# GpSimd's subtraction for the lower parts of the weights: four instructions of 256 columns instead of one of 1024

## The chip, the cores and the metric

The kernel runs on one core of a Trainium2 chip. The metric is device time in microseconds. The kernel before has a median of 3354.24 us over 3 runs (3351.83 to 3357.93).

## The reference

A sequence of 512 tokens with 1024 features passes two blocks of two layers each, all in float32. A layer of block 1 has RMS norms, one wide input product, rotary positions, windowed attention with sinks, compressed, selected and windowed attention with gates, two branch products mixed by gates, an output product with a norm behind it, and a feed-forward with a causal convolution of width 3 over 5632 channels, GELU and gate. A layer of block 2 has a state-space part (a convolution of width 7, a chunked scan in both directions, gate and norm), windowed attention with a relative bias, an output product over both, and a gated feed-forward. What matters here:

```python
def hybrid_layer(x, ...):                       # block 1, called for each of 2 layers
    h = rms_norm(x, attn_pre_gain)
    u = h @ w_in
    ...
    x = x + rms_norm(mixed @ w_out, attn_post_gain)
    h = rms_norm(x, ffn_pre_gain)
    x = x + rms_norm(conv_ffn(h, ffn_w_up, ffn_conv_w, ffn_conv_b, ffn_w_down), ffn_post_gain)
```

## The kernel before

The activations are kept transposed, as tiles of 128 features by 512 tokens. A product of float32 precision is made of three products of a reduced type: each operand is an upper part (`h`, `wh`) and a lower part (`hl`, `wl`), and `mm3` (lines 488 to 490) adds upper by upper, lower weight by upper, upper weight by lower into one bank of PSUM.

The weights come as 460 chunks of 128 x 1024, eight tiles of 128 x 128 each, in the order in which TensorE takes them. The class `Stream` handles them. `load` (line 301) issues a chunk's DMA on the SyncE queue into one of four raw buffers; `conv` makes the upper part by a copy on ScalarE (line 314), or on GpSimd while `busy["act"]` is set, in some stretches with attention (line 312), and then the lower part, raw minus upper, on GpSimd (line 315). Both parts have four buffers. `next` is called for each tile; at the first tile of chunk c it loads up to chunk c + 6 and converts up to chunk c + 3, and it hands slices of 128 columns of both parts to `mm3`.

The order of instructions on every engine is the order in which the program writes them; the waits between engines are put in by the framework. GpSimd's queue holds, beside the chunks, a share of the element-wise work: one tap of the width-7 convolution (line 1410), the scan's decays `adm`, weights `xw` and sums `xd` (lines 1628, 1544, 1643, 1684), rotary products (828), lower parts of some activations (400), and every second residual add behind a norm (1341).

The places that the prediction speaks of: `Squares.add` (line 421, closing add 424) sums the squares of the feature tiles on VectorE; `sums` (433) adds them over the features on TensorE (`stat`); `rstd_a` (442 to 455) takes one over the root by eleven small VectorE instructions of four columns behind a reduction; `spread` (472) broadcasts it to all partitions on TensorE (`statb`). In `dense_group` the squares come while the first products of four output tiles run, and the broadcast comes five weight tiles into the next product. In the convolution of block 2 the taps are the VectorE instructions of line 1416, ScalarE applies the activation (1421) and TensorE transposes the result (`xtp`, 1520). In the scan TensorE makes `gp` (1658), for which a bank has to be free that VectorE reads (`xd`, 1695). In block 1 `sk` (1102), `KL` (639) and `gx` (1181) are VectorE instructions of the attention and of the mixing, and `sp` and `mh` are a product and an operand that come behind such instructions.

Of the kernel before, what the change touches and what calls it, by code (L numbers as in the profile page):

```python
# [10 lines left out]
F32 = mybir.dt.float32  # L11
# [6 lines left out]
T = 512  # L18
# [5 lines left out]
NSLOT = 66              # working tiles of 128 x T  # L24
NB, NO = 2, 2           # output tiles taken together where the last factor comes late
XD = 30                 # tiles of weights before the first heads' queries are split
GA, GB, GC = 1, 4, 1    # tiles of weights before, between and within the gated products
NWU, NKW = 13, 6        # products that keep the clock up: at the start, at a norm
# [6 lines left out]
# ------------------------------------------------------------------ weight stream  # L35
# [8 lines left out]
def _plan():  # L44
    """128x128 weight tiles in the order in which the tensor engine takes them."""
# [103 lines left out]
# ------------------------------------------------------------------ constants of the shapes  # L149
# [37 lines left out]
def _onehot():  # L187
    """Bucket of each relative position -255..255 (t5, bidirectional); row 32 marks the outside."""
    oh = np.zeros((33, 512), np.float32)
    for i in range(512):  # L190
        rel = i - 255
        if i == 511 or abs(rel) > 128:
            oh[32, i] = 1
            continue
        n = abs(rel)
        b = n if n < 8 else 8 + sum(n * n >= 64 * 2 ** k for k in range(1, 8))
        oh[(16 if rel > 0 else 0) + min(b, 15), i] = 1
    return oh
# [48 lines left out]
def trunk_kernel(ctx: ExitStack, tc: tile.TileContext, xT, positions, wts, cst_d, oh_d, rb_d, cw1_d,  # L247
# [20 lines left out]
    # the eight banks of PSUM in turn; a bank that is held stays out until it is free again  # L268
# [16 lines left out]
    # ---------------------------------------------------------------- weights  # L285
    class Stream:
# [18 lines left out]
        def conv(self, upto):  # L305
            while self.conved < min(upto, NCHUNK):
                c = self.conved
                r = self.raw.pop(c)
                h = wpool.tile([128, CH * 128], F32R, tag="wh", name="wh", bufs=4)
                lo = wpool.tile([128, CH * 128], F32R, tag="wl", name="wl", bufs=4)  # L310
                if busy["act"]:
                    G.tensor_copy(h, r)  # L312
                else:
                    A.activation(h, r, AF.Copy)  # L314
                G.tensor_sub(lo, r, h.bitcast(F32))  # L315
                self.hl[c] = (h, lo)
                self.conved += 1

        def defer(self, n, fn):
            """fn after n more tiles of weights."""  # L320
            self.later.append((self.t + n, fn))
# [26 lines left out]
        def drip(self, gen):  # L348
            """One step of gen for each tile of weights from now on."""
            def f():  # L350
                if next(gen, self) is not self:
                    self.defer(1, f)
            self.defer(1, f)
# [3 lines left out]
    # ---------------------------------------------------------------- constants  # L357
# [38 lines left out]
    def split(h, lo, src, eng_l=None, scale=None):  # L396
        """h + lo == src (times the column scale), each in 12 significant bits."""
        if scale is None:
            A.activation(h, src, AF.Copy)  # L399
            (eng_l or V).tensor_sub(lo, src, h.bitcast(F32))  # L400
        else:
            A.activation(h, src, AF.Identity, bias=0.0, scale=scale)  # L402
            V.scalar_tensor_tensor(lo, src, scale, h.bitcast(F32), op0=OP.mult, op1=OP.subtract)  # L403

    class Squares:
        """Squares summed over the feature tiles; the last tile stays one of its own where it comes late."""
# [19 lines left out]
        def sums(self, upto):  # L426
            """The sums over the features of a tile, [token of a block, block], for the tiles that are there."""
# [9 lines left out]
    def rstd_a(sq, n, act=False):  # L437
        """1/sqrt(mean + eps) of each token, [token of a block, block]."""
# [19 lines left out]
    def warm_sqrt():  # L458
        """Brings the table of the square root in ahead of its use."""
        A.activation(small(1, "warm"), epst, AF.Sqrt)  # L460

    def keep_warm(n):
        """Products that keep the tensor engine's clock up while it waits."""
# [4 lines left out]
    def spread(r4):  # L468
        """[token of a block, block] to [any partition, token], in PSUM."""
# [22 lines left out]
    def dense(keys, hs, evac):  # L492
        """One output tile; yields after each tile of the contraction."""
# [12 lines left out]
    def dense_parts(keys, hs, cut, evacs):  # L506
        """Some output tiles: the first part of the contraction for each of them, then the rest."""
# [11 lines left out]
    def dense_group(keys, hs, evacs, sq, store, x=None, after=None):  # L519
        """Four output tiles, the contraction outermost: it starts with the first tile of hs.  The factor of the  # L520
        norm (of the squares sq, of x where they are still to come) and what follows from it come a little into
        the next product."""
# [30 lines left out]
    def prep(x, gcol, late=False):  # L553
        """Gain and split of a tile, and its square for the norm; as a function of the tile's number."""
# [32 lines left out]
    def run_units(units, lags, fill, per, tail=0, prep=()):  # L587
        """Stage k of unit u comes at step u + lags[k]; the filler goes in between (per: steps per unit, tail:
        steps of the filler for each step after the last unit; prep: pieces of work, each with its first step)."""
# [25 lines left out]
    def pieces_of(gen, n):  # L615
        """A generator's n pieces as functions."""
        return [lambda: next(gen, None)] * n

    def stack_q(X, h, get):
        """One of a pair of heads as a tile of its two parts: products over all 128 rows; in two pieces."""  # L620
# [7 lines left out]
    def stack_k(K, g, get):  # L628
        """Keys of one of a pair of groups: their upper part and their lower part, each twice; in four pieces."""
# [19 lines left out]
    def head_units(h, score, ranges, order, vt, o, final):  # L649
        """The four units of a head: the scores of each block of queries; then for each block of keys (ranges: the  # L650
        queries that see it) the probabilities transposed, in two parts, and their product with the two parts of
        the values, side by side, over all those queries at once.  order: the keys, such that each of these
        products either adds to sums of all its queries or, the bank's marks cleared by the first one, starts them
        all.  o["t"][its half] becomes the
        product, [features, tokens]."""
# [57 lines left out]
    def widen(o, den):  # L713
        """A factor of each token, [token of a block, block and head], for each feature."""
# [3 lines left out]
    def spread_pair(o):  # L718
        """A pair of heads, [features, tokens], times their factors."""
# [11 lines left out]
    def value_parts(pt, s, name):  # L731
        """Values of one of a pair of groups, [tokens of a block, block, upper and lower part]."""
# [10 lines left out]
    # ================================================================ block 1  # L743
# [39 lines left out]
    def layer1(l, x, hs, sq, gnext, side):  # L783
# [48 lines left out]
        def tokens(src, name):  # L832
            """[features, tokens] to [tokens of a block, block, features]."""
# [5 lines left out]
        # ---- compressed keys and values  # L839
        cmp = {}  # L840

        def windows(src):
            """The tokens 16 n + 2 i + (0 or 1) of each group of heads, with the position added."""
# [70 lines left out]
        def cmp_scores(i):  # L914
            """Softmax over the compressed blocks, times the gate, transposed; all heads of a block."""
# [42 lines left out]
        def head(src, h):  # L958
            """The two pieces that make head h's tile; the source goes after the second head of the pair."""
# [7 lines left out]
        # ---- projections  # L967
# [63 lines left out]
        # ---- fillers  # L1031
# [20 lines left out]
        # ---- attention units  # L1052
# [10 lines left out]
        def halves(name):  # L1063
            """Half a tile; the other half goes to the next call."""
# [6 lines left out]
        def score_of(h, X, K, mask, k0, init, nm, den, last):  # L1071
            """Exponentials of the scores of a block of queries, not yet normed, and their first block of keys."""
# [16 lines left out]
        # sliding window with sinks  # L1089
# [42 lines left out]
        # selected blocks (all of them are selected) and window, both causal  # L1132
# [41 lines left out]
        # ---- branches, output, post norm  # L1174
# [40 lines left out]
        # ---- feed forward  # L1215
# [85 lines left out]
    def later(i, gated):  # L1301
        """The gated products of the pairs that are there, in steps a little into the products that follow."""
# [4 lines left out]
    class Acts:  # L1307
        """Eleven of the gated products, each taken when it is there."""
# [20 lines left out]
    def post_norm(x, ys, gcol, sq, gnext, side):  # L1329
        """x += norm(ys); its split for the products that follow, and the squares of the norm before them."""  # L1330
# [17 lines left out]
    # ================================================================ block 2  # L1348
    bias_d = dpool.tile([128, 16, 384], F32, name="bias_d")

    def bias_table():
        """Bias by relative position, laid out as [query of a block, head, key of three blocks]."""
# [34 lines left out]
    def layer2(l, x, hs, sq, gnext):  # L1387
# [58 lines left out]
        # ---- dt and decays, [token of a chunk, chunk, direction and head]  # L1446
# [64 lines left out]
        # ---- x to tokens  # L1511
# [46 lines left out]
        # ---- chunked scan, both directions  # L1558
# [38 lines left out]
        def advance(prev, c, g, d, xw):  # L1597
            """State after the chunk from the state before it (None: zero)."""
# [172 lines left out]
        # ---- windowed attention; the state space half of the output product fills in  # L1771
# [69 lines left out]
        # ---- feed forward  # L1841
# [101 lines left out]
    # ================================================================ program  # L1943
# [67 lines left out]
```

## Time and profile before

| | |
|---|---|
| median of 3 runs | 3354.24 us |
| profiled execution, span (its own time) | 3354.5 us |
| TensorE busy (PE) | 3132.5 us, 93%, 14604 products |
| VectorE busy (DVE) | 2145.5 us, 64% |
| ScalarE busy (ACT) | 1465.3 us, 44% |
| GpSimd busy (POOL) | 1539.9 us, 46%, 770 instructions |
| mean granted TensorE clock | 0.967 |

The span goes from the first to the last instruction and is the time of the profiled execution. Busy time is the sum of an engine's instructions; an instruction that stands still for a resource counts as busy. A wait is put down to what released it last.

### The profile page before, as it was taken

Reading aid. Unit: us, or ns where it says so; the run is one execution under the profiler, and the core shown is the slowest. Engines: PE = TensorE matmul, PEld = TensorE weight load, DVE = VectorE, ACT = ScalarE, POOL = GpSimd, SP = SyncE. Lnnn points to the kernel's source line nnn. Section 1 sums busy time; section 2 is a strip of 40 time slices with the busy share of each in tenths; the row PEclk is TensorE's granted clock in tenths of the full one; section 3 lists DMA queues with packets and bytes.
Section 4 is the critical chain, followed back from the end, with each engine's and each line's share of the span. In section 5 each row is a group of like instructions: output and inputs, shape, how many; then the busy total and the mean of one; then the engine's idle time right before and its main releaser. Section 6 shows DMA issues by size and latency. Waiting matters only on the chain. (4 is left out here: it accounts for less than half of the span.)

```text
span 3354.5 us, 39917 instructions
## 1 busy us (share of the span) xinstructions
PE 3132.5 (93%) x14604; PEld 2567.9 (77%) x14604; DVE 2145.5 (64%) x3431; ACT 1465.3 (44%) x2828; POOL 1539.9 (46%) x770
## 2 busy tenths in 40 slices
PE   9989989999989999999888889999998888999998
PEld 7778778887778877888766667888887666788887
DVE  7787467263887747635578987462528898836253
ACT  3357344343246634433345466342333545734232
POOL 4533434554534334544447543354444664335443
PEclk8999999999999999999898899999999989999999
DMA  5311333333521133333321121333332102133332
GB/s 191 101 45 45 101 106 95 107 114 113 164 67 48 48 129 91 102 100 126 104 71 55 46 72 57 109 105 124 93 128 67 57 32 82 57 107 101 126 94 69
DMA packets 104031, 306.05 MB, mean 91 GB/s; under 512 B 12651, under 2 KB 21867, under 8 KB 103836
## 3 DMA queue, kind: packets, MB, share of 16 engines
q1 hardware_dynamic: 103836, 303.50, 28.7%
q8 instruction: 116, 1.90, 0.2%
q14 instruction: 79, 0.65, 0.1%
HBM read 275.64 MB, written 19.96 MB: 88 GB/s over the span
## 5 line engine op out<-in xcount | busy, mean ns | idle before, releaser
L315 POOL TENSOR_TENSOR wl<-wraw,wh 128x1024 fp32r<-128x1024 f32 x460 | 1165.2, 2538 | 1075.6 <-ACT wh L314 1006.4
L488 PE MATMUL acc<-h,wh 128*128 128x512 f32 x2464 | 1005.2, 408 | 0.7 <-ACT h L402 0.7
L489 PE MATMUL acc<-h,wl 128*128 128x512 f32 x2464 | 978.2, 397 | 2.5 <-POOL wl L315 2.5
L490 PE MATMUL acc<-hl,wh 128*128 128x512 f32 x2464 | 976.5, 396 | 0.2
L314 ACT ACTIVATE wh<-wraw 128x1024 fp32r<-128x1024 f32 x400 | 418.9, 1051 | 357.3 <-PE acc L490 257.9
L490 PEld LDWEIGHTS acc<-hl,wh 128*128 128x128 f32 x2464 | 473.1, 192 | 104.7 <-DVE hl L403 1.8
L489 PEld LDWEIGHTS acc<-h,wl 128*128 128x128 f32 x2464 | 474.6, 193 | 98.4 <-POOL wl L315 5.3
L488 PEld LDWEIGHTS acc<-h,wh 128*128 128x128 f32 x2464 | 475.0, 193 | 96.1 <-issue 5.0
L488 PE MATMUL acc<-ah,wh 128*128 128x512 f32 x704 | 274.4, 390 | 0.0
L490 PE MATMUL acc<-al,wh 128*128 128x512 f32 x704 | 274.1, 389 | 0.0
L489 PE MATMUL acc<-ah,wl 128*128 128x512 f32 x704 | 273.9, 389 | 0.0
L673 PE MATMUL pt<-cst,p 128*128 128x128 f32 x752 | 143.1, 279 | 34.1 <-DVE nm L1936 13.4
L1416 DVE SCALAR_TENSOR_TENSOR c<-u,prm,c 128x510 f32<-128x510 f32 (+2 forms) x120 | 147.9, 1233 | 40.8 <-POOL c L1410 37.4
L312 POOL CAST wh<-wraw 128x1024 fp32r<-128x1024 f32 x60 | 70.4, 1173 | 207.7 <-PE acc L490 207.5
L1298 DVE TENSOR_TENSOR al<-c,ah 128x512 fp32r<-128x512 f32 x88 | 118.0, 1341 | 70.8 <-ACT ah L1296 70.8
L490 PEld LDWEIGHTS acc<-al,wh 128*128 128x128 f32 x704 | 132.2, 188 | 28.5 <-DVE al L1298 0.9
L488 PEld LDWEIGHTS acc<-ah,wh 128*128 128x128 f32 x704 | 132.2, 188 | 27.8 <-ACT ah L1296 0.6
L489 PEld LDWEIGHTS acc<-ah,wl 128*128 128x128 f32 x704 | 132.2, 188 | 27.1
L421 DVE TENSOR_TENSOR sq<-sq 128x512 f32<-128x512 f32 x81 | 94.5, 1193 | 89.9 <-ACT sq L416 89.9
L1228 ACT ACTIVATE c<-u,prm 128x512 f32<-128x512 f32 x88 | 71.2, 815 | 163.8 <-DVE u L1224 163.8
L1084 ACT ACTIVATE p<-p,nm 128x128 f32<-128x128 f32 x192 | 102.5, 534 | 90.1 <-DVE nm L1082 88.2
L1296 ACT ACTIVATE ah<-c 128x512 fp32r<-128x512 f32 x88 | 55.5, 630 | 195.3 <-DVE c L1293 195.3
(333 smaller groups left out, 5313.7 us busy)
## 6 DMA issues: line engine op xcount, KB each, us to landing
wraw<-in_wts SPq DMA_DIRECT2D x460, 512.0 KB, 3.6
bias<-bias_d SPq DMA_DIRECT2D x32, 192.0 KB, 2.4
x<-in_xT SPq DMA_DIRECT2D x16, 256.0 KB, 6.1
cw<-in_cw SPq DMA_DIRECT2D x16, 256.0 KB, 4.4
xf<-x SPq DMA_DIRECT2D x16, 256.0 KB, 2.2
x<-xf SPq DMA_DIRECT2D x16, 256.0 KB, 5.6
xs<-x SPq DMA_DIRECT2D x16, 256.0 KB, 3.5
x<-xs SPq DMA_DIRECT2D x16, 256.0 KB, 6.0
```

The costliest lines, as they stand in the source:

```text
L312: G.tensor_copy(h, r)
L314: A.activation(h, r, AF.Copy)
L315: G.tensor_sub(lo, r, h.bitcast(F32))
L421: V.tensor_add(self.p[e], self.p[e], q)
L488: PE.matmul(acc, wh, xh, start=first, stop=False)
L489: PE.matmul(acc, wl, xh, start=False, stop=False)
L490: PE.matmul(acc, wh, xl, start=False, stop=last)
L673: PE.transpose(pt[:, 128 * n:128 * n + 128], t[:, 128 * (kb - b0):128 * (kb - b0) + 128], ident)
L1084: A.activation(p[:, 0:w], p[:, 0:w], AF.Exp, bias=nm[:, col:col + 1], scale=-1.0, accum_out=den[:, col:col + 1])
L1228: A.activation(c, u, AF.Identity, bias=cb[:, idx:idx + 1], scale=cw[:, 88 + idx:89 + idx])
L1298: V.tensor_sub(lo, a, h.bitcast(F32))
L1416: V.scalar_tensor_tensor(c[:, lo:hi], u[:, lo + d:hi + d], cw[:, 12 * k + idx:12 * k + idx + 1], c[:, lo:hi], op0=OP.mult, op1=OP.add)
```

## The change

Line 315, one subtraction for a chunk's 1024 columns, becomes a loop of four subtractions of 256 columns each, in order. Operands, results and the place in the queue are the same. The rest of the diff takes comments and docstrings out.

```diff
@@ class Stream, conv
                 else:
                     A.activation(h, r, AF.Copy)
-                G.tensor_sub(lo, r, h.bitcast(F32))
+                for q in range(4):
+                    s = slice(256 * q, 256 * q + 256)
+                    G.tensor_sub(lo[:, s], r[:, s], h[:, s].bitcast(F32))
                 self.hl[c] = (h, lo)
                 self.conved += 1
```

## Rows read from the trace of the kernel before

**Rows 1.** the page: engine totals; line: busy us, mean ns, idle before

```profile
PE 3132.5 (93%) x14604; PEld 2567.9 (77%) x14604; DVE 2145.5 (64%) x3431; ACT 1465.3 (44%) x2828; POOL 1539.9 (46%) x770
...
L315 POOL TENSOR_TENSOR wl<-wraw,wh 128x1024 fp32r<-128x1024 f32 x460 | 1165.2, 2538 | 1075.6 <-ACT wh L314 1006.4
```

**Rows 2.** waits of TensorE: who waited for whom, total us, times, longest

```profile
PE xtp L1520 <- ACT c L1421: 28.0, 10, 7.8
...
PE stat L433 <- DVE sq L424: 26.7, 6, 7.5
...
PE gp L1658 <- DVE xd L1695: 21.2, 4, 8.2
...
PE acc L488 <- ACT mh L399: 9.6, 6, 3.4
...
PE sp L646 <- DVE gx L1037: 4.7, 2, 2.3
...
PE acc L489 <- POOL wl L315: 2.5, 6, 0.8
```

**Rows 3.** line 1298, a VectorE subtraction: min/median/max ns

```profile
L1298 DVE TENSOR_TENSOR al<-c,ah x88: 691/694/2886, 496.2 to 3283.4; 128x512 fp32r<-128x512 f32 x88
```

**Rows 4.** timeline of GpSimd, undisturbed series: start us, us, instruction, count

```profile
116.49 5.04 POOL L828 TENSOR_TENSOR swap<-swap,sinT 128x512 f32<-128x512 f32 x4
...
610.60 9.46 POOL L315 TENSOR_TENSOR wl<-wraw,wh 128x1024 fp32r<-128x1024 f32 x4 [3.03 <-ACT wh L314]
```

**Rows 5.** timeline of GpSimd, 456 to 467 us, three of four subtractions

```profile
456.14 2.79 POOL L315 TENSOR_TENSOR wl<-wraw,wh 128x1024 fp32r<-128x1024 f32 x1 [0.63 <-ACT wh L314]
...
461.70 2.78 POOL L315 TENSOR_TENSOR wl<-wraw,wh 128x1024 fp32r<-128x1024 f32 x1
...
464.45 2.78 POOL L315 TENSOR_TENSOR wl<-wraw,wh 128x1024 fp32r<-128x1024 f32 x1
```

**Rows 6.** timeline of VectorE, 456 to 473 us

```profile
456.59 2.90 DVE L421 TENSOR_TENSOR sq<-sq 128x512 f32<-128x512 f32 x1
...
470.66 0.17 DVE L450 TENSOR_SCALAR var<-var 128x4 f32<-128x4 f32 x1
...
472.64 0.16 DVE L455 SCALAR_TENSOR_TENSOR rs<-rt,rs 128x4 f32<-128x4 f32 x1
```

**Rows 7.** timeline of TensorE, 468 to 477 us

```profile
468.56 1.87 PE L433 MATMUL stat<-ones,sq 128*128 128x1 f32 x8 [7.44 <-DVE sq L424]
...
476.59 0.60 PE L472 MATMUL statb<-cst,rs 128*128 128x128 f32 x4
```

**Rows 8.** windows, 470.3 to 476.3 us: busy us by engine, clock, DMA

```profile
470.30:476.30 6.00, 6.00 (x15) 4.74 (x16) 1.97 (x12) 0.00 (x0) 0.00 (x0) 0.50 0.00 0
```

**Rows 9.** timeline of GpSimd, 848 to 853 us

```profile
848.53 4.69 POOL L315 TENSOR_TENSOR wl<-wraw,wh 128x1024 fp32r<-128x1024 f32 x2 [3.31 <-ACT wh L314]
```

**Rows 10.** timeline of VectorE, 851 us

```profile
850.96 2.29 DVE L451 TENSOR_SCALAR rs<-var 128x4 int32<-128x4 int32 x1
```

**Rows 11.** timeline of VectorE at three places

```profile
177.98 2.22 DVE L1102 TENSOR_TENSOR sk<-nm,nsink 128x8 f32<-128x8 f32 x1
...
222.04 2.00 DVE L639 CAST KL<-KL 64x512 fp32r<-64x512 f32 x1
...
382.00 2.56 DVE L1181 TENSOR_TENSOR gx<-gx 128x512 f32<-128x512 f32 x1
```

**Rows 12.** timeline of GpSimd, 1733 us

```profile
1732.58 2.35 POOL L315 TENSOR_TENSOR wl<-wraw,wh 128x1024 fp32r<-128x1024 f32 x1
```

**Rows 13.** timeline of VectorE, 1733 to 1739 us

```profile
1732.66 5.96 DVE L1416 SCALAR_TENSOR_TENSOR c<-u,prm,c 128x510 f32<-128x510 f32 x5 [2.46 <-POOL c L1410]
```

**Rows 14.** windows of line 315 alone: convolution, then scan, one layer

```profile
1665.00:1790.00 125.00, 39.40 (x16) 0.95 0.20 62
1790.00:1910.00 120.00, 20.30 (x9) 0.89 0.13 42
```

**Rows 15.** windows of all engines, the scan

```profile
1790.00:1910.00 120.00, 99.44 (x406) 73.10 (x404) 112.92 (x160) 66.78 (x187) 86.02 (x67) 0.89 0.13 42
```

## The prediction, made before the changed kernel ran

> **What bounds the kernel now.** I read the page's engine totals first: TensorE is busy for 93% of the span and GpSimd for 46% [rows 1]. The 460 subtractions hold GpSimd for 1165 us, but its idle time before them is nearly as long, so GpSimd as a whole is no bound. Next the list of waits of TensorE alone: it waited 2.5 us in all for the lower parts [rows 2]. A lower part that is ready sooner is therefore worth at most about that. The long waits there are for VectorE or for what follows it: the sums of squares, the short convolutions, the scan's `gp`, `mh` and `sp`. So I asked how GpSimd's subtraction touches VectorE. One VectorE subtraction with two SBUF operands takes 691 ns at least, 694 in the median and 2886 at most [rows 3]; the excess, 2.2 us, is close to one GpSimd instruction. The timelines show the mechanism: a sum of squares begun at 456.59 ends at 459.49, 0.56 us behind the end of the subtraction that began at 456.14 [rows 5, 6]. VectorE's instruction stands still until GpSimd's ends, gets in at that boundary, and the next subtraction is stretched: two that follow each other with a sum between them start 2.75 us apart [rows 5], four undisturbed ones take 9.46, so 2.365 each [rows 4]. A handover costs GpSimd 0.39 us, and VectorE never waits for more than one GpSimd instruction.
>
> So the change moves no work from TensorE. It gives VectorE four boundaries per chunk instead of one.
>
> **The new instruction.** No row has 256 columns. Subtractions' spacing is 2.365 us for 1024 columns; four products of 512 columns take 5.04, so 1.26 each [rows 4]. The line through both has 1.105 us per 512 columns and 0.155 fixed, so 256 columns take 0.71. Bounds: 0.59, a quarter of 2.365 with nothing fixed, and 1.26, since 256 columns should not take longer than 512. I take 0.71, as it is worked from both rows. A chunk then costs 2.84 instead of 2.365 us, 0.47 more, and 460 of them 218 us: GpSimd goes from 1540 to some 1760 us busy, 52%. Idle time hides it; without that cover a chunk would be late by 0.47 us, and TensorE's wait in rows 2 shows that this cover fails six times now. The Trainium skill's GPSIMD Engine Reference, section 3.1, gives 2.6 cycles per element at 1.2 GHz and tens of cycles for dispatch: an estimate from that page is 0.6 us for 256 columns, and by it the time forecast below would be some 8 us shorter.
>
> **Three norms before a feed-forward or a new block (468, 1275 and 1659 us, one pattern).** Four subtractions follow each other from 456.14, and five sums of squares have to pass, one per instruction; TensorE waits 7.44 us for them, until 468.56 [rows 5 to 7]. After the change: the first piece starts 0.39 late as now and ends at 457.28; the first sum ends 0.56 later, at 457.84; the others follow at 0.71 + 0.39 = 1.10, so the fourth at 461.14 and the closing one at 462.24. The sums start at 462.3, 6.3 us sooner.
>
> What is late next: the reciprocal root, eleven VectorE instructions of four columns, from 470.66 to 472.80 [rows 6], 2.1 us after the sums' start; GpSimd is quiet there now. After the change they begin at 464.4, while GpSimd has 16 × 0.71 + 6 × 0.39 = 13.7 us of work from 456.14, until 469.8. Two subtractions back to back with these instructions in wait take 4.69 us, and the second such instruction takes 2.29 [rows 9, 10]: one of the chain per GpSimd instruction, and no stretch for GpSimd. So seven or eight of the eleven take 0.71 each until 469.8, the rest 0.20 each: done at 470.5, broadcast at 470.6 instead of 476.59 [rows 7], 6.0 us sooner. Now the stretch between ran at a granted clock of 0.50, the 1.2 GHz level, 15 products in 6.0 us [rows 8]; at the upper level it needs about half, so TensorE would reach the broadcast at about 467.5 and wait 3 us there. If the clock falls behind that wait as it did behind the 7.44 us one, about 2.8 us are given back. Between 3.2 and 6.0 I take 4 each: 12 us. A fourth norm (848 us) has two subtractions in the chain itself [rows 9, 10]; there one wait becomes several short ones, and I count nothing.
>
> **Single instructions caught ahead of TensorE.** `sk` takes 2.22 us, the cast of `KL` 2.00, `gx` at 382 us 2.56 [rows 11]; TensorE waits behind them (`sp` for `gx`: 4.7 us in two; `mh`: 9.6 in six) [rows 2]. At worst each waits for one whole piece, 0.75: the two short ones end within 0.78 us, and `gx`, with 0.56 behind the boundary, within 1.3. Savings 1.45, 1.2 and 1.25; both layers of block 1 run the same code, so twice: 7.8 us.
>
> **Dense VectorE chains.** In the convolution five instructions stand in a row: the subtraction ends at 1734.93, the chain, begun at 1732.66, at 1738.62 [rows 12, 13]; behind the first one four take 0.785 each, so one subtraction costs the chain 2.85 − 0.785 = 2.07 us. In pieces, every piece gets between two of them: 4 × (0.71 + 0.39 − 0.785) = 1.26. That is 0.8 less. Of ten `xtp` waits, 28.0 us [rows 2], six have a subtraction in the chain: 4 us, as part of what is won waits elsewhere. In the scan VectorE is busy for 112.9 of 120 us and holds 9 subtractions a layer [rows 14, 15]; its instructions of 128 columns would be let through one per piece, 0.71 instead of some 0.3 us (estimated from the 0.69 for 512 columns in rows 3), 1.6 per chunk against up to 2.1 now, while GpSimd's own work behind it comes 0.47 later: 0, between −4 and +9 for 18 chunks.
>
> **Waits added.** TensorE's second product of a tile can now have to wait at each quarter of a chunk, up to 1380 more semaphore waits; behind such a wait stand all later products. Chunks are converted three ahead, so the piece is long there. The first tiles of a late chunk need only the first piece: 1 us of the 2.5 in rows 2; were each to wait for all four, it would be 3 us slower. No DMA is added; the raw buffer is free 0.47 us or a few handovers later, while TensorE needs about 5 us for a chunk (24 products at half of the 0.40 of rows 8).
>
> **Sum.** 12 + 7.8 + 4 + 0 + 1 = 25 us off the profiled execution's 3354.5, which is also within 0.3 us of the median 3354.24: 3329.
>
> **Rivals.** *Given back in the norms.* If short VectorE instructions also cost GpSimd 0.39 at each handover, the root's chain ends 3 to 4 us later and the clock falls twice: the norms are worth 0, the dense chains too, the single ones partly: 3349. For it: eleven dependent instructions stand exactly where the pieces are. Against it: 4.69 us for two subtractions [rows 9], with no stretch. Chance 0.18.
> *More than counted.* The clock stays up behind the shorter waits (6.0 a norm, 18 in all), pieces near 0.6 us, dense chains win 1 us each: 45 off, 3309. For it: the shorter waits are under half of 7.44 us; against it: they don't vanish. Chance 0.17.
> *Slower: the dense stages pay per piece.* In convolution and scan 50 chunks stand in two layers [rows 14], VectorE there is the chain that TensorE waits for (`xtp` 28.0, `gp` 21.2) [rows 2]. From 4 × (q + 0.39 − 0.785) = 2.07, so a piece of q = 0.91 us, each chunk costs that chain more than now. At q = 1.1 it is 0.75 × 50 = 38 more, the norms win nothing since GpSimd's queue lasts until 476, the single ones 6: +32, 3386. For it: nothing in the trace prices 256 columns, and 1.26 is the upper bound; against it: the line through two sizes. Chance 0.15.
> That the pieces don't act singly (a reader waiting for all four) would change only the 1 us above.
>
> **How the numbers follow.** Forecast 3329, chance 0.50 (its own spread 3315 to 3345). The range 3302 to 3362 takes in the larger gain, the return to no change, and pieces up to about 1.0 us in the dense stages. A measurement tells 0.2%, 6.7 us, from no change. Faster: nearly all of the forecast and of the larger gain and a little of the first rival, 0.70; same: most of that rival, 0.14; slower 0.16.
>
> **What would show it.** Pieces spaced 0.6 to 0.8 us; VectorE's subtraction of 512 columns at most about 1.4 us instead of 2.9; sums at about 462 us, the root's chain stretched to some 6 us, the broadcast at 470 to 471; `sp` no longer waiting 2.3 us for `gx`; scan stages of unchanged length. Pieces above 0.9 us, or a scan longer by several us, would make the prediction wrong.

## The result, and the profile after

The kernel after takes 3277.06 us (median; 3273.16 to 3278.73), the kernel before beside it 3354.31: a ratio of 0.977, 95% interval 0.9756 to 0.9784. The change takes off 77 us. The forecast was 3329, 25 us off, in a range from 3302 to 3362; the sign was right, the size was a third of what came, and the time lies below the range.

The page of the kernel after: span, busy time of each engine, and the line of the new instruction (busy us, mean ns, idle before it).

```profile
span 3271.4 us, 41483 instructions
...
PE 3099.8 (95%) x14604; PEld 2548.7 (78%) x14604; DVE 1944.4 (59%) x3431; ACT 1467.1 (45%) x2828; POOL 1884.2 (58%) x2150
...
L317 POOL TENSOR_TENSOR wl<-wraw,wh 128x256 fp32r<-128x256 f32 x1840 | 1508.3, 852 | 770.7 <-ACT wh L314 725.7
```

Against [rows 1], GpSimd is busy for 344 us more. VectorE executes the same 3431 instructions and is busy for 201 us less: time in which it stood still before. The profiled span is 83 us shorter. TensorE executes the same 14604 products and is busy for 33 us less, at a mean granted clock of 0.978 instead of 0.967. So of the 83 us some 50 are waits of TensorE that are gone, and 33 are products that ran faster. (Line numbers from 315 on are higher by 2 than before.)

The waits of TensorE before that [rows 2] do not show, in the same columns:

```profile
PE gnt L1024 <- DVE gn L811: 10.1, 2, 5.0
...
PE yp L1693 <- DVE dm L1671: 6.8, 4, 2.2
PE statb L472 <- DVE rs L455: 6.4, 5, 2.6
PE pt L673 <- ACT p L1084: 6.1, 4, 2.6
PE ops L691 <- DVE pth L683: 5.9, 6, 1.4
```

The waits of TensorE after:

```profile
PE xtp L1522 <- ACT c L1423: 21.8, 8, 6.6
PE gp L1660 <- DVE xd L1697: 19.9, 4, 7.1
...
PE stat L435 <- DVE sq L426: 13.1, 8, 2.7
PE statb L474 <- DVE rs L457: 12.0, 10, 3.3
PE gnt L1026 <- DVE gn L813: 6.7, 2, 3.4
...
PE gp L1660 <- POOL adm L1630: 5.1, 9, 1.3
...
PE acc L490 <- ACT mh L401: 3.0, 2, 1.6
...
PE pt L675 <- ACT p L1086: 3.0, 4, 1.0
...
PE sp L648 <- DVE gx L1039: 1.4, 2, 0.7
...
PE ops L693 <- DVE pth L685: 1.2, 2, 0.6
...
PE yp L1695 <- DVE dm L1673: 0.8, 2, 0.5
```

Against [rows 2], `stat` went from 26.7 to 13.1 us, `mh` from 9.6 to 3.0, `xtp` from 28.0 to 21.8, `sp` for `gx` from 4.7 to 1.4. The wait for the lower parts (2.5 us) is gone. Longer are `statb` (6.4 to 12.0) and `gp` for GpSimd's own `adm` (1.3 to 5.1). Shorter as well are waits in block 1's attention (`gnt`, `pt`, `ops`) and in the scan (`yp`) that the prediction does not name.

**The first norm.** Timeline of GpSimd after (start us, us, instruction, count): a chunk whose pieces no VectorE instruction stretches, and the norm.

```profile
154.98 2.83 POOL L317 TENSOR_TENSOR wl<-wraw,wh 128x256 fp32r<-128x256 f32 x4
...
433.28 12.88 POOL L317 TENSOR_TENSOR wl<-wraw,wh 128x256 fp32r<-128x256 f32 x14 [1.84 <-ACT wh L314]
```

Timeline of VectorE after, in the same norm:

```profile
434.74 6.94 DVE L423 TENSOR_TENSOR sq<-sq 128x512 f32<-128x512 f32 x6 [1.76 <-ACT sq L418]
441.72 1.10 DVE L426 TENSOR_TENSOR sq<-sq 128x512 f32<-128x512 f32 x1
444.52 0.16 DVE L444 TENSOR_REDUCE var<-stat 128x4 f32<-128x4 f32 x1 [1.70 <-PE stat L435]
...
444.92 0.58 DVE L453 TENSOR_SCALAR rs<-var 128x4 int32<-128x4 int32 x1
445.54 0.64 DVE L455 TENSOR_TENSOR rt<-rs 128x4 f32<-128x4 f32 x1
...
450.54 0.16 DVE L457 SCALAR_TENSOR_TENSOR rs<-rt,rs 128x4 f32<-128x4 f32 x1
```

Timeline of TensorE after:

```profile
442.87 1.61 PE L435 MATMUL stat<-ones,sq 128*128 128x1 f32 x8 [2.31 <-DVE sq L426]
...
450.84 0.62 PE L474 MATMUL statb<-cst,rs 128*128 128x128 f32 x4 [0.19 <-DVE rs L457]
```

Windows of all engines after, from the sums to the broadcast (columns as in [rows 8]):

```profile
443.00:450.00 7.00, 7.00 (x21) 5.78 (x22) 5.17 (x10) 0.00 (x0) 7.00 (x11) 0.51 0.53 173
```

A sum of squares takes 1.16 us instead of 2.8 [rows 5, 6], one per piece. TensorE waits 2.31 instead of 7.44 us [rows 7]. Most of the root's instructions take about 0.65 instead of 0.16 us, so that the broadcast comes 8.0 us behind the sums. TensorE hardly waits for it (0.19 us): it ran the products in between at a granted clock of 0.51, the 1.2 GHz level, as before [rows 8], though the wait ahead of them was a third as long.

**Block 1.** Line 1181 (`gx`) of the kernel before: count and min/median/max ns.

```profile
L1181 DVE TENSOR_TENSOR gx<-gx x16: 692/1135/2615, 360.8 to 1193.4; 128x512 f32<-128x512 f32 x16
```

The same instruction after:

```profile
L1183 DVE TENSOR_TENSOR gx<-gx x16: 691/692/958, 344.6 to 1149.4; 128x512 f32<-128x512 f32 x16
```

There are 16 such instructions, and several were caught, not one per layer. A second example is a small one that the prediction did not list, ahead of products of the attention. Timeline of VectorE, before:

```profile
162.28 1.82 DVE L1107 TENSOR_TENSOR den<-den,sk 128x8 f32<-128x8 f32 x1
```

And after:

```profile
154.44 0.48 DVE L1109 TENSOR_TENSOR den<-den,sk 128x8 f32<-128x8 f32 x1
```

**A chain of the convolution.** Timeline of VectorE after, the chain of [rows 13]:

```profile
1670.16 5.37 DVE L1418 SCALAR_TENSOR_TENSOR c<-u,prm,c 128x510 f32<-128x510 f32 x5 [2.46 <-POOL c L1412]
```

It is 0.59 us shorter; the four pieces beside it take 4.12 us instead of 2.35 [rows 12].

### The profile page after: what moved, and what is told of

Its sections match the earlier page's. It is cut to its first block, busy times and chain, and to the rows that moved or that the text cites. A ratio compares the mean times of both kernels' runs of the same rounds, so it can differ in the third digit from the quotient of the medians.

```text
span 3271.4 us, 41483 instructions
## 1 busy us (share of the span) xinstructions
PE 3099.8 (95%) x14604; PEld 2548.7 (78%) x14604; DVE 1944.4 (59%) x3431; ACT 1467.1 (45%) x2828; POOL 1884.2 (58%) x2150
## 5 line engine op out<-in xcount | busy, mean ns | idle before, releaser
L317 POOL TENSOR_TENSOR wl<-wraw,wh 128x256 fp32r<-128x256 f32 x1840 | 1508.3, 852 | 770.7 <-ACT wh L314 725.7
L1226 DVE TENSOR_TENSOR u<-acc,R 128x512 f32<-128x512 f32 x88 | 59.7, 684 | 157.6 <-PE acc L492 157.5
L1418 DVE SCALAR_TENSOR_TENSOR c<-u,prm,c 128x510 f32<-128x510 f32 (+2 forms) x120 | 128.9, 1074 | 40.8 <-POOL c L1412 37.4
L1300 DVE TENSOR_TENSOR al<-c,ah 128x512 fp32r<-128x512 f32 x88 | 100.7, 1145 | 68.7 <-ACT ah L1298 68.7
L402 POOL TENSOR_TENSOR ol<-ot,oh 128x512 fp32r<-128x512 f32 x32 | 41.4, 1294 | 166.3 <-ACT oh L401 166.3
```

Of the source, the lines that this page charges most:

```text
L317: G.tensor_sub(lo[:, s], r[:, s], h[:, s].bitcast(F32))
L1226: V.tensor_mul(u, acc, st3["R"])
L1300: V.tensor_sub(lo, a, h.bitcast(F32))
L1418: V.scalar_tensor_tensor(c[:, lo:hi], u[:, lo + d:hi + d], cw[:, 12 * k + idx:12 * k + idx + 1], c[:, lo:hi], op0=OP.mult, op1=OP.add)
```

## The experiments

The theory, called "ports" in the expectations: a VectorE instruction with two SBUF operands (some with one, too) that meets a GpSimd instruction stands until that one ends; shorter GpSimd instructions make each such wait shorter, and TensorE gets what stands in its chains. Rivals: the lower parts or the buffers come free earlier; or the gain is a shift in time that does not belong to any stage. In each comparison the kernel before ran beside on the same chip (3352.5, 3355.1, 3354.0 and 3352.9 us in the four groups). A gain in us carries some 4 us of uncertainty, a difference of two gains some 6.

**e1, the pieces in reverse order.**

```diff
-                for q in range(4):
+                for q in (3, 2, 1, 0):
```

> The four pieces are issued last quarter first; each piece is as long as in the changed kernel, but a chunk's first tile (its first quarter) now has its lower part only with the fourth piece. Theory 'ports': VectorE instructions with two SBUF inputs wait only for the GpSimd instruction under way, so only the length of the pieces counts: 3277 us, within 5. Rival 'earlier release': the gain comes from TensorE's first tiles, the buffers and the transfers being let go after a quarter of a chunk: then the first tile waits as long as before or longer, 3340 to 3360 us, and TensorE's list of waits names GpSimd's lower part.

3284.95 us, ratio 0.9801 (0.9788 to 0.9814). Of the 77 us some 67 stay although the first quarter now comes last. The rest is the order of the pieces, a little more than the 5 us allowed; the wait for the lower parts is back:

```profile
PE acc L491 <- POOL wl L317: 6.1, 4, 1.8
```

So the earlier release of first tiles is worth at most 10 us, and the length of the instruction the rest.

**e2 and e3, two and eight pieces.**

```diff
-                for q in range(4):
-                    s = slice(256 * q, 256 * q + 256)
+                for q in range(2):                          # e2
+                    s = slice(512 * q, 512 * q + 512)
+                for q in range(8):                          # e3
+                    s = slice(128 * q, 128 * q + 128)
```

> Two pieces of 512 columns, spaced 1.25 us; a chunk costs GpSimd 2.5 us. Theory 'ports': a VectorE instruction that comes at a random moment waits half a piece, 1.18 us in the kernel before, 0.63 here, 0.36 with four pieces; the gain of 77 us, taken in these proportions, is 51 here: 3303 us, between 3293 and 3315. By the steps that the prediction counted alone (norms, six single instructions, convolution) it would be about 3335. If what matters is that there are boundaries at all and not the length between them: 3280 or less.

> Eight pieces of 128 columns, spaced 0.43 us by the line through 1024 and 512 columns (0.155 fixed); a chunk costs 3.45 us, GpSimd's busy time rises by some 280 us. Theory 'ports' without a price of the boundaries: a mean wait of 0.22 instead of 0.36 us, 90 us off the kernel before: 3264. With the price (0.39 us of GpSimd and up to 0.5 us of VectorE per boundary in dense chains, where eight pieces now stand in the chain instead of four): 3270 to 3300. A time above 3300 would say that boundaries cost more than the rows show.

e2: 3313.53 us, ratio 0.9888 (0.9874 to 0.9901), 39 off. e3: 3229.26, ratio 0.9637 (0.9624 to 0.965), 123 off. From the page of e2, busy time of each engine:

```profile
PE 3115.5 (94%) x14604; PEld 2561.1 (77%) x14604; DVE 2044.6 (62%) x3431; ACT 1465.9 (44%) x2828; POOL 1677.5 (51%) x1230
```

And of e3:

```profile
PE 3084.8 (96%) x14604; PEld 2534.6 (79%) x14604; DVE 1893.4 (59%) x3431; ACT 1467.9 (45%) x2828; POOL 2191.4 (68%) x3990
```

VectorE's busy time falls by 101, 201 and 252 us for two, four and eight pieces; the time by 39, 77 and 123. The expectations by mean waits were off in opposite directions, two pieces by 10 us (inside its range), eight by 35: the steps from one piece on win 39, 38 and 46 us, they do not shrink with the mean wait. One reason is in the chains. Where dependent VectorE instructions follow each other, each gets in behind one piece, so four pieces only hand the chain the old wait in parts; half as long pieces halve it. Timeline of VectorE in e3, the root's chain of the first norm:

```profile
443.10 0.38 DVE L455 TENSOR_TENSOR rt<-rs 128x4 f32<-128x4 f32 x1
443.52 0.39 DVE L456 SCALAR_TENSOR_TENSOR rt<-rt,var 128x4 f32<-128x4 f32 x1
```

0.16 us undisturbed, 0.65 beside pieces of 256 columns, 0.38 beside pieces of 128. In the two scan stages, where VectorE is busy almost throughout [rows 15], the same products take 242.9 us before, 241.3 with four pieces and 227.2 with eight, and the last step is all waits of TensorE, whose products keep their time (193.3 and 193.5 us).

The other reason is TensorE's clock. Windows of all engines over the same 63 products of the first norm, after and in e3:

```profile
435.63:454.52 18.89, 16.40 (x63) 12.97 (x62) 15.94 (x24) 7.15 (x11) 14.65 (x17) 0.82 0.43 139
435.55:450.64 15.09, 13.19 (x63) 10.51 (x62) 12.33 (x23) 7.15 (x11) 15.09 (x31) 1.00 0.37 105
```

In e3 TensorE waits 0.63 us ahead of the sums instead of 2.31, and the clock does not fall: 3.2 of the 3.8 us are faster products. Over the three norms eight pieces win 10.8 us more than four, 9.2 of them in the products' own time. Which share of the 46 us each reason has in the other stages was not tested.

**e4, the root of the norm with operands in PSUM** (the small tiles lie in the held bank of the sums; every instruction has one operand at most from SBUF).

```diff
-        v = small(4, "var")
+        v = small(4, "var") if act else ps[:, 256:260]
...
-        t4 = small(4, "rt")
+        t4 = ps[:, 260:264]
...
-            V.tensor_mul(t4, r4, r4)
-            V.scalar_tensor_tensor(t4, t4, -0.5, v, op0=OP.mult, op1=OP.mult)
+            V.tensor_mul(t4, r4, v)
+            V.scalar_tensor_tensor(t4, t4, -0.5, r4, op0=OP.mult, op1=OP.mult)
```

> As the changed kernel, but the reciprocal root of a norm keeps its mean square and its products in the held PSUM bank, so that each of its eleven VectorE instructions reads at most one operand from SBUF. Theory 'ports': they no longer wait for GpSimd's pieces (0.65 to 0.69 us each after the change, about 0.2 without GpSimd): 11 x 0.45 = 5 us less in each of four norms, of which TensorE's wait for the broadcast can give at most 12 us in all: 3265 to 3270 us. Rival: the chain is as long as its own instructions and their waits for each other, whatever GpSimd does: 3277, or slower by what PSUM operands cost.

3261.31 us, ratio 0.9729 (0.9716 to 0.9742): 16 us less than the changed kernel by the medians, 12 by the profiled spans, slightly more than expected. Timeline of VectorE, the same chain, and of GpSimd beside it:

```profile
441.81 0.17 DVE L455 TENSOR_TENSOR stat<-rs,stat 128x4 f32<-128x4 f32 x1
...
442.22 0.16 DVE L457 SCALAR_TENSOR_TENSOR rs<-stat,rs 128x4 f32<-128x4 f32 x1
```

```profile
429.96 16.32 POOL L317 TENSOR_TENSOR wl<-wraw,wh 128x256 fp32r<-128x256 f32 x19 [1.84 <-ACT wh L314]
```

Beside the same pieces each instruction takes 0.17 us: what made it 0.65 was its second SBUF operand, not its dependence. The Trainium skill's "SBUF — State Buffer", section "SBUF: two separate sides", names two SBUF inputs as a case in which VectorE and GpSimd exclude each other; this trace agrees (0.65 against 0.17 us). That does not clear every instruction with a single SBUF operand: L453 has one and took 0.58 us after the change, and the cast of `KL` took 2.00 [rows 11].

**e5 to e7, four pieces in one group of chunks only.** The edit of e5; e6 and e7 differ in the names.

```diff
+                n = PLAN[c * CH][0]
+                w = 256 if n in ("w_in", "w_branch_a", "w_branch_b", "w_out") else 1024
+                for q in range(0, CH * 128, w):
+                    G.tensor_sub(lo[:, q:q + w], r[:, q:q + w], h[:, q:q + w].bitcast(F32))
```

> Four pieces only for the 98 chunks of block 1's projections, branches and output product (w_in, w_branch_a, w_branch_b, w_out of both layers); all other chunks in one instruction as before. Theory 'many small links': laid product by product beside the kernel before, the changed kernel gains 37 us in the stretches where these chunks are subtracted, most of it in attention at places that the prediction didn't count: 37 us off, 3316 (3310 to 3323). By the prediction's terms (six single instructions 7.8, first tiles 0.5) it would be 8 off, 3346. If a gain in one stage is only a shift that another stage's subtractions make possible, the three kernels e5, e6 and e7 don't add up to the whole 77.

> Four pieces only for the 98 chunks of block 2's projections and output product (w_in_2, w_out_2 of both layers), which are subtracted in the norm at 1659 us, the convolution, the scan and the windowed attention. Theory 'many small links': 28 us off (norm 5, convolution 18, scan 4): 3326 (3319 to 3333). By the prediction's terms (one norm 4, convolution 4, scan 0): 8 off, 3346.

> Four pieces only for the 264 chunks of the feed-forwards; among them those that are subtracted during the norms at 468 and 1275 us. Theory 'many small links': 6 and 5 us in these norms, 4 elsewhere: 15 off, 3339 (3333 to 3345), though more than half of all chunks are in it, since TensorE hardly waits for VectorE in a feed-forward. By the prediction's terms (two norms of 4): 8 off, 3346.

e5: 3315.43 us, ratio 0.988 (0.9865 to 0.9895), 39.7 off. e6: 3326.27, 0.9912 (0.9898 to 0.9925), 28.9 off. e7: 3342.88, 0.996 (0.9947 to 0.9972), 12.3 off. All three lie inside the ranges expected. The sum is 80.9 against 77: the parts add up, so the gain belongs to stages and is no shift. Half of it stands in the 98 chunks of block 1 and about a sixth in the 264 of the feed-forwards.

**e8, no subtraction.** The kernel leaves the weights' lower part out of the result; TensorE's products are as many.

```diff
-                lo = wpool.tile([128, CH * 128], F32R, tag="wl", name="wl", bufs=4)
...
-                for q in range(4):
-                    s = slice(256 * q, 256 * q + 256)
-                    G.tensor_sub(lo[:, s], r[:, s], h[:, s].bitcast(F32))
-                self.hl[c] = (h, lo)
+                self.hl[c] = (h, h)
```

> No subtraction of weights on GpSimd at all: the second product of each tile takes the upper part of the weights in place of the lower part, so the lower part's share is left out of the result; TensorE's products are as many. It prices all that the subtraction costs TensorE. Across one, two, four and eight instructions per chunk the excess of VectorE's instructions over the shortest of their kind was 570, 471, 362 and 281 us, and the gain 0, 39, 77 and 123 us: 0.37 to 0.43 us per us of excess removed. Theory 'ports': the excess falls to the part that comes from GpSimd's other work (perhaps 100 us), so 170 to 200 us off the kernel before: 3155 to 3185. Rival: the waits that are left belong to the chains themselves, and eight pieces already have nearly all: 3210 to 3230.

3146.32 us, ratio 0.9375 (0.9363 to 0.9388), 209 off, a little more than expected. Page:

```profile
PE 3056.8 (97%) x14604; PEld 2523.5 (80%) x14604; DVE 1720.9 (55%) x3431; ACT 1466.1 (47%) x2828; POOL 376.8 (12%) x310
```

So in the kernel before the subtraction cost TensorE 209 us, of which its own list of waits named 2.5 as waits for lower parts. 76 of the 209 us are no waits at all: the products' own time falls from 3132.5 to 3056.8 us, at a mean clock of 0.992. Four pieces win 37% of the 209.

**e9 and e10, the chunks of three norms, and of the convolution.** The edit of e9; e10 has `239 <= c <= 254 or 354 <= c <= 369`.

```diff
+                w = 256 if 52 <= c <= 56 or 167 <= c <= 171 or 234 <= c <= 238 else 1024
```

> Four pieces only for the 15 chunks that are subtracted during the norms at 468, 1275 and 1659 us (five each). Prediction's term: 12 us off (4 a norm, after 2 us each for the clock): 3342. Product by product the changed kernel gained 5.1, 5.9 and 4.75 us at these sums and lost 0.3, 0.3 and 0.9 at the broadcasts: 14 off, 3340 (3337 to 3344). Both stand close; only below 7 or above 20 off would the alignment be misleading.

> Four pieces only for the 32 chunks that are subtracted during the two convolution stages (16 each). Prediction's term: 0.8 us at each of six waits, 4 off: 3350. Theory 'every link counts' (chains of VectorE instructions, each caught at most once per GpSimd instruction, and TensorE behind most of them): 9.0 and 9.1 us in these stages, 18 off: 3336 (3330 to 3342).

e9: 3335.55 us, ratio 0.9945 (0.9933 to 0.9957), 18.5 off. e10: 3340.39, 0.9958 (0.9947 to 0.997), 13.6 off. Both are above the prediction's terms (12 and 4); in e10 the alignment of the traces was too high by 4, in e9 too low by 4 (1 us outside the range given), which is the uncertainty of these differences. Windows over the same 449 products of the first convolution stage, before and in e10:

```profile
1670.19:1790.16 119.97, 102.75 (x449) 82.34 (x448) 92.05 (x102) 53.52 (x99) 56.67 (x31) 0.94 0.21 65
1668.25:1780.88 112.63, 100.18 (x449) 80.52 (x448) 84.70 (x102) 53.80 (x100) 77.36 (x75) 0.97 0.21 67
```

Of the 7.3 us 2.6 are faster products. In the second stage it is 5.1 of 7.4, at a clock of 0.97 instead of 0.93. In e10's list of waits `xtp` falls from 28.0 to 24.0 us, and `btp`, another transposition behind the same instructions, from 3.8 to 0.7.

**e11 and e12, eight and sixteen pieces with the root in PSUM.** The edit of e12 against e4 (e11 has 8 and 128 in place of 16 and 64):

```diff
-                for q in range(4):
-                    s = slice(256 * q, 256 * q + 256)
+                for q in range(16):
+                    s = slice(64 * q, 64 * q + 64)
```

> Eight pieces of 128 columns together with the root's operands in PSUM. Alone they gave 3229 and, on four pieces, 15.7 us off 3277. With eight pieces a step of the root's chain waits 0.4 instead of 0.7 us, so the second edit has less to take: 6 to 10 off, 3219 to 3223. If the two took the same time, 3229; if they add, 3213.

> Sixteen pieces of 64 columns and the root in PSUM. The spacings measured, 0.70 us for 256 columns and 0.42 for 128, put 64 at 0.28: 4.5 us of GpSimd per chunk where TensorE takes about 4.9 to use one, GpSimd's busy time about 2700 us, 84%. Theory 'ports': VectorE's waits shrink again (0.14 us on average), 20 to 35 us more: about 3195; but in the stages where GpSimd has work of its own (convolution, scan) the chunks then come late and TensorE waits for the lower parts, up to 1 us for each of 82 chunks. I expect the two to cancel: 3205 to 3235, with GpSimd's lower part back in TensorE's list of waits.

e11: 3222.49 us, ratio 0.9612 (0.9599 to 0.9624), as expected, the fastest kernel here: 55 us below the changed one by the medians. e12: 3326.83, ratio 0.9921 (0.9903 to 0.9938), 104 us slower than e11 and far above what I expected. Page and waits of e12:

```profile
PE 3120.9 (94%) x14604; PEld 2538.3 (76%) x14604; DVE 1948.7 (59%) x3431; ACT 1466.9 (44%) x2828; POOL 2815.1 (85%) x7670
```

```profile
PE xtp L1523 <- ACT c L1424: 38.1, 13, 5.4
...
PE gp L1661 <- POOL adm L1631: 21.5, 22, 5.7
...
PE acc L492 <- POOL wl L317: 10.2, 33, 0.6
```

GpSimd is nearly full (85%), and its own work comes late behind the pieces: `gp` waits 21.5 us for `adm` (12.7 in e11), and VectorE 70.3 us for the tap of the convolution (40.8 in e11), with `xtp` behind it. The lower parts themselves are the smaller wait, 10.2 us in 33; I had expected them to be the main one. 37 of the 100 us between the profiled spans of e12 and e11 are again the products' own time (3083.5 us in e11).

**e13 to e15, block 1 in three parts.** The edit of e14; e13 has `c <= 18 or 115 <= c <= 133`, e15 `41 <= c <= 48 or 154 <= c <= 163`.

```diff
+                w = 256 if 19 <= c <= 40 or 134 <= c <= 153 else 1024
```

> Four pieces only for the first 19 chunks of each layer of block 1 (projections up to the start of the sliding-window attention, 38 chunks). The prediction counted nothing here. Theory 'every link counts': of e5's gain product by product some 12 us stand in these stretches (gnt 1.7 in each layer, the rest at the start and the first hidden product): 12 off, 3342 (3337 to 3346). Rival: the part at the start is scatter of the first loads, and 5 off remain: 3349.

> Four pieces only for the 42 chunks subtracted during block 1's attention. The prediction counted sk and KL, 1.45 and 1.2 us, once per layer: 5 off, 3349. Theory 'every link counts': five places of TensorE per layer of 1.1 to 1.6 us each (products with vaT and vwT, two scores, a transposition): 16 off, 3338 (3333 to 3342).

> Four pieces only for the 18 chunks subtracted while the branches are summed and multiplied with the output weights. The prediction counted one gx per layer, 1.25 us: 2.5 off, 3351.5. Theory 'every link counts': in each layer TensorE's wait for mh goes from 4.8 to 1.5 us because two or more of the eight gx are caught per layer, and other places with it: 10 off, 3344 (3340 to 3347). The three kernels e13, e14 and e15 should add up to e5's 39.7.

e13: 3349.58 us, ratio 0.9987 (0.9978 to 0.9995), 3.3 off, near the rival's 5: what the two traces showed at the start was mostly scatter, and the expectation missed. e14: 3332.04, 0.9938 (0.9924 to 0.9951), 20.8 off, 1 us beyond its range. e15: 3342.57, 0.9971 (0.996 to 0.9982), 10.3 off. Together 34.4, within the uncertainty of e5's 39.7. Waits of TensorE in e15:

```profile
PE acc L490 <- ACT mh L401: 3.0, 2, 1.5
```

The wait for `mh`, 9.6 us in [rows 2], falls to 3.0 with these 18 chunks alone. In e14 `gnt` falls to 7.0 us, `pt` for `p` (line 1086) to 3.0, `ops` for `pth` to 1.2 and `sp` for `gx` to 1.4. Windows over the same 1247 products of the attention in the first layer, before and in e14:

```profile
125.00:365.10 240.10, 223.55 (x1247) 189.51 (x1246) 185.88 (x466) 142.43 (x383) 87.64 (x53) 0.97 0.15 49
124.93:352.43 227.50, 219.03 (x1247) 187.34 (x1246) 172.10 (x465) 142.51 (x384) 101.12 (x117) 0.98 0.16 51
```

Of the 12.6 us 8.1 are waits and 4.5 faster products.

## Why the prediction was wrong in size

**What held.** The mechanism: e1, e4 and e8 leave no room for another as the main cause. The piece: 2.83 us for four, 0.71 each, as worked out. The Trainium skill's GPSIMD Engine Reference, section 3.1, has 2.6 cycles per element for two inputs; the trace agrees, since 2.365 less 0.71 us over 768 columns is 2.15 ns a column, by the page's 1.2 GHz an estimate of 2.6 cycles. The 0.6 us that I had estimated from the page was too low by the fixed part of an instruction, 0.155 us in the prediction's line. The spacing with a handover: 1.16 us against 1.10. The sums of the first norm: a wait 5.1 us shorter against 6.3. The root's chain stretched to 6.0 us, as forecast. VectorE's subtraction of 512 columns takes 1268 ns at most, where 1.4 us was forecast and [rows 3] have 2886, though its median went from 694 to 1144. The convolution's chain: 0.6 us shorter against 0.8. So the prices of these single events were right within a quarter of a microsecond, the norm's sums aside. GpSimd's own price was not: 344 us more busy time instead of 218, since handovers stretch the pieces: 1508.3 us for 1840 are 202 above 0.71 each, where the 460 subtractions before were 77 above 2.365 each. TensorE felt little of it, 3.8 us more for `adm`.

By kind of wait the forecast came close, too. The waits that it named (`stat`, `xtp`, `gp` for `xd`, `mh`, `sp`, lower parts) fell by 33.5 us, and `statb` and `adm` grew by 9.4: 24 net, against a forecast of 25. That the two meet so closely is luck, since the single terms were off in both directions.

**What failed: the term "single instructions caught ahead of TensorE", 7.8 us.** It priced three instructions and doubled them for the two layers. In block 1 outside the norms the runs measured 34 us by parts (e13 to e15) or 39.7 at once (e5). The attention alone has 20.8 where I put 5.3 (`sk`, `KL`), and the branch sums 10.3 where I put 2.5 (`gx`). I had taken three examples out of a timeline for the population. Line 1181 shows 16 instructions with a median of 1135 ns over a minimum of 692; the small `den` of line 1107, 1.82 us instead of 0.48 after, wasn't in my list at all. Laid product by product beside the kernel before, e14 wins 1.1 to 1.6 us at each of five places per layer (`gnt`, two of `ops`, `sp`, `pt`), some 15 us in all: about what I had counted per link, but not their number. [rows 2] show none of `gnt`, `pt` and `ops`, 22 us of waits; over the whole kernel the waits that I had not named fell by 26 us.

**What had no term: TensorE's clock outside the norms.** I counted only waits. With the waits shorter the granted clock rose, and the same products took 33 us less, 40% of the gain by the spans: in the attention 8.7 of 24.0 us (e14, both layers), in the convolution 7.6 of 14.7 (e10). 24 us of waits named, 26 not named and 33 in the clock make the 83. Which wait brought the clock back up in which stretch was not taken apart.

**The convolution, 4 us: 13.6 (e10).** The wait that I had priced was right: `xtp` fell by 4.0 us. Left out were `btp`, 3.1 us, and the clock, 7.6.

**The norms, 12 us: 18.5 (e9).** I took 2 us off each norm because TensorE, at the upper clock level, would reach the broadcast early and wait 3 us. It reached it as the root came: the wait is 0.19 us, because the clock fell behind the shorter wait too (0.51 in the window above). The whole shift of the sums stayed. What I had forecast here happened in e1: there TensorE waited 0.73 us ahead of the sums, the clock from the sums to the broadcast was 0.89, and TensorE reached the broadcast early and waited 3.39 us for it.

**The scan, 0: not settled.** The rest of e6, 28.9 less 13.6 and a third of e9's 18.5, leaves 9 us for scan and windowed attention together, with an uncertainty of some 6. Over the same products the two scan stages together take 241.3 instead of 242.9 us after the change, which is close to the 0. No run splits these chunks alone.

**The first tiles, 1 us.** e1 lost 8 to 10 us of the gain by the reversed order. Part of that is a first tile that waits longer there than behind one instruction (2.84 against 2.365 us), so the early release itself is worth less than that; the list of waits puts it at 2.5 us (2.5 before, none after, 6.1 in e1). No run parts the two.

**The rivals.** "Given back in the norms" fell: no stretch of GpSimd by short instructions showed, and e9 is positive. "Slower: the dense stages pay per piece" fell at its own condition: 0.71 us against the 0.91 from which it would have decided. "More than counted" came nearest. Its 18 us for the norms are what e9 shows (18.5), but by luck: its condition was a clock that stays up behind the shorter waits, and in the first norm it fell. With eight pieces the condition holds (1.00 in e3). The pieces were not near 0.6 us, and the clock's larger part, in the attention and the convolution, was missing there as well.

The total could have warned me: in the trace before, VectorE's instructions take some 570 us more in all than the shortest of their kind, and 425 us of its busy time go with the subtractions (e8). Each us taken off VectorE went with 0.38 to 0.49 us of the whole time in e2, the change, e3 and e8. A forecast of 25 us for a change that cuts the wait per instruction by two thirds should have been held against that sum. The two signs of being wrong that I had named, slow pieces and a longer scan, looked for a smaller gain alone.

## What to carry to other kernels

Where GpSimd and VectorE exclude each other, the length of one GpSimd instruction sets the wait of every VectorE instruction that meets it; cut it into pieces as short as GpSimd's free time pays for (eight here; sixteen filled GpSimd and lost 104 us against eight), and keep operands of short dependent chains in PSUM. When a mechanism is found at one instruction, price it over all instructions of its kind, by a row that groups them (count, minimum, median, maximum), not over the few that a timeline happened to show. Ask also what shorter waits do to TensorE's clock: compare its busy time for the same products, and not only its waits. Then hold the sum against the total that the mechanism can cost.

## What was not expected of the hardware

The gain did not flatten with shorter pieces: 39, 38 and 46 us for each halving down to 128 columns. A chain of dependent VectorE instructions takes one piece per link, so its length follows the piece (0.65, then 0.38 us per link), until GpSimd itself has no time left (sixteen pieces, 85% busy). With eight pieces the clock also stayed at the upper level in all three norms, where it had fallen with four (1.00 against 0.82 to 0.88 over the windows of the norms).

A VectorE instruction of two operands beside the same pieces takes 0.17 us when only one of them comes from SBUF (e4).

TensorE's clock fell behind a wait of 2.31 us as it had behind one of 7.44: 0.51 in the 7 us after the sums. Behind 0.63 us (e3) it did not fall.
